# Sums of squares with four columns of ones, and residual products with both halves of the activations in 512 columns

## Chip, core and metric

The kernel runs on one NeuronCore of a Trainium2 chip, as one launch. The metric is the device time of a run in microseconds. In the profile PE is the matrix engine, PEld its loads of the stationary operand, DVE, ACT and POOL the vector, scalar and general engines, SP the engine that issues nearly all transfers.

## What is computed

Two transformer blocks over 256 tokens of 1024 features, in fp32. The first has two layers, each with a feed-forward part, an attention (differential in layer 0, forgetting in layer 1) and a second feed-forward part, all of them added to x with gates from a conditioning vector. The second block adds convolution mixers, a cross-attention to 256 memory tokens and a layer of 16384 experts chosen by product keys. What matters here, cut from the reference:

```python
def rms_norm(x, g):
    y = xf * lax.rsqrt(jnp.mean(xf * xf, axis=-1, keepdims=True) + EPS)
...
def swiglu(h, w_in, w_out):
    g, u = jnp.split(h @ w_in, 2, axis=-1)
    return (jax.nn.silu(g) * u) @ w_out
...
        x = x + 0.5 * g1[:, None, :] * swiglu(h, ffn_w_in[layer, 0], ffn_w_out[layer, 0])
        h = modulate(rms_norm(x, norm_g[layer, 1]), sh2, sc2)
...
        x = x + g2[:, None, :] * mix        # mix ends in  o @ w_o
        h = modulate(rms_norm(x, norm_g[layer, 2]), sh3, sc3)
        x = x + 0.5 * g3[:, None, :] * swiglu(h, ffn_w_in[layer, 1], ffn_w_out[layer, 1])
...
    merged = jax.nn.sigmoid(gate_sc) * y_sc + jax.nn.sigmoid(gate_cf) * y_cf
    return jnp.einsum('bsd,de->bse', merged, w_mix_out)
```

So each product with an output weight (w_out, w_o, w_mix_out, w_xo) is added to x, and the mean square of the new x over its 1024 features is needed before the next norm.

## The kernel before

x lies feature-major in xT, eight tiles of 128 features by 256 tokens. Weights come once each, in chunks of [128, 2048] fp32 (1 MB) into `raw`. Each half of a chunk is split into a rounded part `whi` by ACT (L115) and the remainder `wlo` by DVE (L116), four buffers of each. Activations are kept as such pairs too. A product is `mm3` (L146 to 149): whi with the rounded activations, whi with their remainder, wlo with the rounded ones, each a matmul of 256 columns into one PSUM bank, the weights being the stationary operand.

An output tile n of ffn_out takes 22 such triples (one for each tile of the 2816 hidden features); of a_w_o, b_w_o, w_mix_out and w_xo it takes 8. `residual` (L425) then makes one DVE instruction that multiplies the bank by the gate and adds it to xT (L426); `residual2` (L784) adds without a gate. Behind it `Stat.add` (L180) squares the new tile on ACT (sq, L182), and `Norm.add` (L235) makes the next norm's input: hi on ACT (L237), lo on DVE (L238).

`Stat` sums squares over features. Seven of the eight squared tiles are added up by POOL (sqa, six adds, L193). Then PE multiplies that sum, and after it the eighth tile, with ones (L177): the squares are the stationary operand, 128 columns of ones the moving one, and the first matmul takes 256 columns to clear the bank. The result has tokens on the partitions, the same value in all columns; column 0 alone is read (L198). There are nine such Stats: one behind each residual projection and a second one in the last ffn. Three Stats (memory, first x, convolution LayerNorm) have `on_pe` and send all eight tiles to PE. From the sums come rstd on ACT and DVE, a transposition on PE (`along_row`, L215, tile pt) and the scaling of the norm (L264). The first products behind a residual (`Norm.pair`, L246) use the unscaled input, so that they need not wait for rstd.

In differential attention TF is a Toeplitz tile of the relative bias: eight transfers (L588) read shifted windows of `gneg`, and PE flips them in pairs of heads (L610) before the scores. Beside all that DVE and ACT work off modulation products (araw, L358) as background.

The order of instructions on each engine is set by the framework's scheduler, which goes by its own estimate of durations; each engine then takes its row in that order and waits where an operand is late. PSUM banks and tile buffers rotate in pools.

Of the kernel before, what the change touches and what calls it, by code (L numbers as in the profile page):

```python
# [27 lines left out]
NB = 32  # L28
LAM0 = 0.8 - 0.6 * math.exp(-0.3 * 0)

# ---- columns of the packed per-feature vectors: name -> (first column, count)
# [22 lines left out]
def forward(ctx: ExitStack, tc: tile.TileContext, io, out, tap=None):  # L54
# [21 lines left out]
    # ---------------------------------------------------------------- constants  # L76
# [15 lines left out]
    # ---------------------------------------------------------------- weights  # L92
    class Weights:
        """Streams [128, 2048] chunks; each gives two pieces split exactly into hi + lo."""
# [5 lines left out]
        def pieces(self, src, n=2048, whole=(), loads=1):  # L100
            """whole: pieces that stay plain fp32, for PE's own (slower) fp32 product."""
# [43 lines left out]
    def mm3(o, a, b, start, stop):  # L145
        """o += a.T @ b for operands split into (hi, lo)."""  # L146
        pe.matmul(o, a[0], b[0], start=start, stop=False)  # L147
        pe.matmul(o, a[0], b[1], start=False, stop=False)  # L148
        pe.matmul(o, a[1], b[0], start=False, stop=stop)  # L149

    def tok(h, k, a=0, b=T):
        """tokens a .. b of feature tile k."""
        return h[0][:, k, a:b], h[1][:, k, a:b]
# [4 lines left out]
    def split_into(pair_hi, pair_lo, src, func=AF.Copy, **kw):  # L158
        """exact hi + lo of src (an fp32 SBUF tile)."""
# [3 lines left out]
    # ---------------------------------------------------------------- norms  # L163
    class Stat:
        """Sum of squares over the features: tokens on partitions, then 1 / rms again along the row."""

        def __init__(self, on_pe=False):
            self.ps = bank("po", [128, 2, 128])
# [4 lines left out]
        def sum(self, sq, first, last_):  # L173
            # the first product also clears the other half of the bank
            for t in range(2):
                o, b = (self.ps, ones0) if first and t == 0 else (self.ps[:, t, :], ones)
# [3 lines left out]
        def add(self, ap, scale=1.0):  # L180
# [5 lines left out]
            elif self.k == KT:  # L186
                self.sum(self.acc, True, False)
                self.sum(sq, False, True)
# [13 lines left out]
        def rstd_after(self, r1):  # L202
            """1 / rms of the rows that r1 scales."""
# [7 lines left out]
    def along_row(r):  # L211
        """[token, 2] -> the same values along the tokens of every partition."""
# [9 lines left out]
    class Norm:  # L222
        """h = (src * a) * r + b in hi + lo, in place of src * a, which the first products take:
        they need no r, which is multiplied into what they give (two more columns carry b)."""
# [21 lines left out]
        def pair(self, p0, p1, keep=None):  # L246
            """two output tiles [128, T] in SBUF; then h is what it should be."""
# [29 lines left out]
    def fm_pair(p0, p1, h):  # L277
        """two feature-major output tiles [128, T]; k outermost."""
# [31 lines left out]

    def proj_tm(W, src, h, dst, scale=None):
        """token-major projection of one chunk (256 columns): dst [128, 2, 256]."""
# [13 lines left out]
    # ---------------------------------------------------------------- inputs  # L326
# [20 lines left out]
    # ---------------------------------------------------------------- modulation  # L347
# [45 lines left out]
    # ---------------------------------------------------------------- memory keys and values  # L393
# [31 lines left out]
    def residual(n, o, s, st, norm):  # L425
        dve.scalar_tensor_tensor(xT[:, n, :], o, s, xT[:, n, :], op0=ALU.mult, op1=ALU.add)  # L426
# [3 lines left out]
    # ---------------------------------------------------------------- feed-forward  # L430
# [872 lines left out]
```

## Time and profile before

| what | before |
|---|---|
| median of 3 runs (lowest, highest), us | 2296.33 (2295.49, 2296.72) |
| span of the profiled execution, us | 2292.8 |
| PE busy, share of the span | 98% |
| DVE, ACT, POOL busy | 76%, 55%, 3% |
| DMA | 461.26 MB read, 202 GB/s over the span |
| lines 147, 148, 149 (mm3) in the chain that ended last | 22% each |

The span is that of one profiled execution; the time of a run holds a few microseconds around it. A matmul's duration is modelled and overlaps with the next one's, so the distance from start to start counts, not the duration. A timeline row joins neighbours that are alike: it gives the first start, the time from there to the last end, and the count. The bracket at the end of a row is the idle time of the engine ahead of it and what ended it. In the busy-time view PEclk is the granted clock as a share of full speed.

### The profile page before, as it was taken

How to read it: one execution, taken by the hardware profiler on the slowest of the kernel's cores; microseconds unless marked ns; L12 is line 12 of the kernel's file. 1: busy time of each engine (PE TensorE's matmuls, PEld its weight loads, DVE VectorE, ACT ScalarE, POOL GpSimd, SP SyncE). 2: the span in 40 equal slices, each digit the busy share in tenths (PEclk: the TensorE clock that was granted, in tenths of full speed). 3: DMA queues.
4: the chain of work that ended last, by engine and by line, in shares of the span. 5: the costliest groups of instructions: out<-in, count | busy, mean ns of one | idle time of the engine just before them, and what ended most of it. 6: DMA issues, size and time to landing. Idle time of an engine off the chain costs nothing.

```text
span 2292.8 us, 42711 instructions
## 1 busy us (share of the span) xinstructions
PE 2235.5 (98%) x16756; PEld 2133.5 (93%) x16756; DVE 1739.7 (76%) x3503; ACT 1257.1 (55%) x2389; POOL 72.0 (3%) x75
## 2 busy tenths in 40 slices
PE   8999869999999999999999999999999999999998
PEld 8999858999999999999999999999999999888886
DVE  7877727977877777855699886899668998666665
ACT  5544538644564447644533455545567776555554
POOL 0000100100200010100100000000000000000000
PEclk9999979999999999999999999999999999999999
DMA  9777664677667773455444543245543444555554
GB/s 367 297 295 294 208 138 170 234 299 279 230 266 297 293 292 129 169 202 183 167 164 166 184 181 151 95 184 184 184 166 132 145 148 148 184 190 194 185 185 155
DMA packets 66489, 466.15 MB, mean 203 GB/s; under 512 B 7472, under 2 KB 8944, under 8 KB 10480
## 3 DMA queue, kind: packets, MB, share of 16 engines
q1 hardware_dynamic: 66000, 462.90, 55.4%
q8 instruction: 132, 2.16, 0.4%
q14 instruction: 69, 0.57, 0.1%
q10 hardware_dynamic: 288, 0.52, 0.1%
HBM read 461.26 MB, written 1.05 MB: 202 GB/s over the span
## 4 chain that ended last, share of the span: by engine, by line
PE 90%; DVE 3%; ACT 3%; issue 1%; SPq 1%; DMA 1%; POOL 0%; DVEq 0%; ACTq 0%; POOLq 0%
PE mm L149 22%; PE mm L147 22%; PE mm L148 22%; PE mm L1164 8%; PE lg L1164 8%; PE lg L1114 2%; PE mm L289 2%; SPq L588 1%; PE po L177 1%; DVE wlo L116 1%; ACT whi L115 1%; DMA TF<-gneg 1%; DVE lo L275 0%; DVE lo L238 0%; DVE nt L270 0%
## 5 line engine op out<-in xcount | busy, mean ns | idle before, releaser
L116 DVE TENSOR_TENSOR wlo<-raw,whi 128x1024 fp32r<-128x1024 f32 x696 | 850.1, 1226 | 325.2 <-ACT whi L115 323.7
L115 ACT ACTIVATE whi<-raw 128x1024 fp32r<-128x1024 f32 x696 | 734.3, 1059 | 617.9 <-PE mm L148 411.9
L147 PE MATMUL mm<-hi,whi 128*128 128x256 f32 x3144 | 899.3, 287 | 0.9 <-ACT hi L274 0.6
L149 PE MATMUL mm<-hi,wlo 128*128 128x256 f32 x3144 | 891.7, 284 | 1.4 <-DVE wlo L116 1.1
L148 PE MATMUL mm<-lo,whi 128*128 128x256 f32 x3144 | 886.1, 282 | 0.6 <-DVE lo L275 0.5
L149 PEld LDWEIGHTS mm<-hi,wlo 128*128 128x128 f32 x3144 | 595.4, 189 | 3.0 <-DVE wlo L116 2.7
L148 PEld LDWEIGHTS mm<-lo,whi 128*128 128x128 f32 x3144 | 595.6, 189 | 2.6 <-DVE lo L275 1.2
L147 PEld LDWEIGHTS mm<-hi,whi 128*128 128x128 f32 x3144 | 594.4, 189 | 2.6 <-ACT hi L274 0.8
L149 PE MATMUL mm<-ghi,wlo 128*128 128x256 f32 x704 | 197.7, 281 | 0.0
L147 PE MATMUL mm<-ghi,whi 128*128 128x256 f32 x704 | 197.7, 281 | 0.0
L148 PE MATMUL mm<-glo,whi 128*128 128x256 f32 x704 | 197.7, 281 | 0.0
L358 DVE CUSTOM_DVE_ANT_0 araw<-araw,cb 128x1024 f32<-128x1024 f32 x160 | 190.3, 1218 | 1.0 <-ACT cb L407 1.0
L160 ACT ACTIVATE vph<-S 128x128 fp32r<-128x128 f32 x256 | 77.1, 302 | 133.0 <-PE lg L1164 132.9
L148 PEld LDWEIGHTS mm<-glo,whi 128*128 128x128 f32 x704 | 132.8, 189 | 0.0
L147 PEld LDWEIGHTS mm<-ghi,whi 128*128 128x128 f32 x704 | 132.8, 189 | 0.0
L149 PEld LDWEIGHTS mm<-ghi,wlo 128*128 128x128 f32 x704 | 132.8, 189 | 0.0
L161 DVE TENSOR_TENSOR vpl<-S,vph 128x128 fp32r<-128x128 f32 x256 | 73.5, 288 | 44.3 <-PE lg L1164 44.2
L812 DVE SCALAR_TENSOR_TENSOR cfc<-cf,vec,cfc 128x256 f32<-128x256 f32 x240 | 99.1, 472 | 0.0
L1106 DVE TENSOR_SCALAR ohA<-cst,sel 128x128 f32<-128x128 f32 x256 | 82.2, 342 | 21.8 <-PE lg L1114 20.9
L1164 PE MATMUL mm<-whi,vph 128*128 128x512 f32 x256 | 80.3, 395 | 0.2 <-ACT vph L160 0.2
L1164 PE MATMUL lg<-whi,vpl 128*128 128x512 f32 x256 | 80.5, 395 | 0.0
L1164 PE MATMUL mm<-wlo,vph 128*128 128x512 f32 x256 | 80.5, 395 | 0.0
(387 smaller groups left out, 3279.7 us busy)
## 6 DMA issues: line engine op xcount, KB each, us to landing
raw<-ffn_in SPq DMA_DIRECT2D x88, 1024.0 KB, 4.8
araw<-ada SPq DMA_DIRECT2D x72, 1024.0 KB, 6.8
raw<-peer_u SPq DMA_DIRECT2D x64, 1024.0 KB, 4.8
raw<-peer_v SPq DMA_DIRECT2D x64, 1024.0 KB, 4.8
raw<-ffn_out SPq DMA_DIRECT2D x44, 1024.0 KB, 4.8
araw<-kv_ada SPq DMA_DIRECT2D x8, 1024.0 KB, 6.9
raw<-w_cf SPq DMA_DIRECT2D x8, 1024.0 KB, 4.8
raw<-w_scx SPq DMA_DIRECT2D x8, 1024.0 KB, 4.8
```

Source lines behind the costliest of these rows:

```text
L115: act.activation(hi[:, :m], r, AF.Copy)
L116: last_split[0] = dve.tensor_tensor(lo[:, :m], r, hi[:, :m], op=ALU.subtract)
L147: pe.matmul(o, a[0], b[0], start=start, stop=False)
L148: pe.matmul(o, a[0], b[1], start=False, stop=False)
L149: pe.matmul(o, a[1], b[0], start=False, stop=stop)
L160: act.activation(pair_hi, src, func, **kw)
L161: dve.tensor_tensor(pair_lo, src, pair_hi, op=ALU.subtract)
L289: pe.matmul(o, p[0][:, k * 128:(k + 1) * 128], h32[:, k, :], start=(k == 0), stop=(k == KT - 1))
L358: dve.tensor_tensor_reduce(out=raw[:, i, :], in0=raw[:, i, :], in1=cb, scale=1.0, scalar=0.0, op0=ALU.mult, op1=ALU.add, accum_out=acc[:, ...
L812: dve.scalar_tensor_tensor(o, cf[:, i, j:j + T], w, o, op0=ALU.mult, op1=ALU.add)
L1106: dve.tensor_scalar(A, iota, sel3[:, 0, t:t + 1], sel3[:, 2, t:t + 1], op0=ALU.is_equal, op1=ALU.mult)
L1164: pe.matmul(acc[t][d], lh, rh[:, d * 512:(d + 1) * 512], start=s0, stop=s1)
```

## The change

Sums: the moving operand of a sum has NS = 4 columns of ones (8 in the first matmul, four of them zero) where it had 128 (256). In Stats without on_pe POOL adds up only the first five squared tiles (four adds); tiles 5, 6 and 7 go to PE one by one, so there are 8 matmuls to a Stat instead of 4.

Products: where a projection is added to x, rounded part and remainder of an activation tile now lie side by side (tiles g, oh2, mx), and `mm_wide` gives whi a moving operand of 512 columns, rounded part and remainder, into the two halves of a bank; wlo with the rounded part (256 columns) goes into the first half. `residual` and `residual2` add the two halves to xT one after the other: 48 more instructions of L426's kind and 16 more of L784's. w_mix_out's first two tiles are interleaved, as `proj_fm` did with wide=True. Some tiles are packed otherwise and TF is allocated larger to fit oh2's buffer; the rest of the computation stays.

```diff
+NS = 4
+DIRECT = 5
@@ Stat
-            self.ps = bank("po", [128, 2, 128])
+            self.ps = bank("po", [128, 2, NS])
...
-                o, b = (self.ps, ones0) if first and t == 0 else (self.ps[:, t, :], ones)
+                o, b = (self.ps, ones0[:, 128 - NS:128 + NS]) if first and t == 0 else (
+                    self.ps[:, t, :], ones[:, :NS])
...
-            elif self.k == KT:
-                self.sum(self.acc, True, False)
-                self.sum(sq, False, True)
+            elif self.k > DIRECT:
+                if self.k == DIRECT + 1:
+                    self.sum(self.acc, True, False)
+                self.sum(sq, False, self.k == KT)
@@ new
+    def mm_wide(o, a, b, first, last):
+
+        def cross():
+            pe.matmul(o[:, 0, :], a[1], b[:, 0, :], start=False, stop=False, skip_group_check=True)
+
+        if not first:
+            cross()
+        pe.matmul(o, a[0], b, start=first, stop=last, skip_group_check=True)
+        if first:
+            cross()
@@ new
+    def proj_wide(W, name, g, consume, together=False):
+
+        src = io[name]
+        for c in range(src.shape[0]):
+            it = W.pieces(src[c])
+            if together and c == 0:
+                p = [next(it), next(it)]
+                o = [mm_bank([128, 2, T]) for _ in p]
+                for k in range(KT):
+                    for oo, pp in zip(o, p):
+                        mm_wide(oo, blk(pp, k), g[:, k], k == 0, k == KT - 1)
+                for i in range(2):
+                    consume(2 * c + i, o[i])
+            else:
+                for i, p in enumerate(it):
+                    o = mm_bank([128, 2, T])
+                    for k in range(KT):
+                        mm_wide(o, blk(p, k), g[:, k], k == 0, k == KT - 1)
+                    consume(2 * c + i, o)
+            tick()
@@ residual
-        dve.scalar_tensor_tensor(xT[:, n, :], o, s, xT[:, n, :], op0=ALU.mult, op1=ALU.add)
+        for i in range(2):
+            dve.scalar_tensor_tensor(xT[:, n, :], o[:, i, :], s, xT[:, n, :], op0=ALU.mult, op1=ALU.add)
@@ ffn
-            ghi = fp.tile([128, FKT, T], F32R, name="ghi")
-            glo = fp.tile([128, FKT, T], F32R, name="glo")
+            g = fp.tile([128, FKT, 2, T], F32R, name="g")
...
-                split_into(ghi[:, j, :], glo[:, j, :], pr)
+                split_into(g[:, j, 0, :], g[:, j, 1, :], pr)
...
-                    mm3(o, next(wb), (ghi[:, k, :], glo[:, k, :]), k == 0, k == FKT - 1)
+                    mm_wide(o, next(wb), g[:, k], k == 0, k == FKT - 1)
@@ differential attention
-        proj_fm(W, "a_w_o", (ohi, olo), lambda n, o: residual(n, o, s[:, n:n + 1], st, norm))
+        proj_wide(W, "a_w_o", oh2, lambda n, o: residual(n, o, s[:, n:n + 1], st, norm))
@@ forgetting attention
-        proj_fm(W, "b_w_o", (ohi, olo), lambda n, o: residual(n, o, s[:, n:n + 1], st, norm))
+        proj_wide(W, "b_w_o", oh2, lambda n, o: residual(n, o, s[:, n:n + 1], st, norm))
@@ residual2
-        dve.tensor_tensor(xT[:, n, :], o, xT[:, n, :], op=ALU.add)
+        for i in range(2):
+            dve.tensor_tensor(xT[:, n, :], o[:, i, :], xT[:, n, :], op=ALU.add)
@@ convolution mixers, cross-attention
-        proj_fm(W, "w_mix_out", (mhi, mlo), lambda n, o: residual2(n, o, st, norm), wide=True)
+        proj_wide(W, "w_mix_out", mx, lambda n, o: residual2(n, o, st, norm), together=True)
...
-        proj_fm(W, "w_xo", (ohi, olo), lambda n, o: residual2(n, o, st, norm))
+        proj_wide(W, "w_xo", oh2, lambda n, o: residual2(n, o, st, norm))
```

The scheduler's order shifts in places. Line numbers in the rows of the changed kernel are its own: L107 is there what L105 was, L118 what L116, L253 what L238, L394 what L358, L463 what L426, L623 what L588; L156 is the 256-column matmul of mm_wide, L160 the one of 512.

SP's row in differential attention, before and then changed; TF are the transfers of the relative bias, raw the weight chunks.

```order
L105 DMA raw<-a_q 128x2048
L355 DMA araw<-ada 128x2048
L105 DMA raw<-a_k 128x2048
L588 DMA TF<-gneg 128x1x256 x8
L105 DMA raw<-a_v 128x2048
```

```order
L107 DMA raw<-a_q 128x2048
L391 DMA araw<-ada 128x2048
L623 DMA TF<-gneg 128x1x256 x8
L107 DMA raw<-a_k 128x2048
L107 DMA raw<-a_v 128x2048
```

The eight TF transfers have moved ahead of the a_k chunk, which now stands between them and a_v.

DVE's row in a_w_o up to the weight split for output tile 6, the last row of each; ahead of the first piece stand two L426 rows and one split of this projection, ahead of the second five L463 rows, one split and two of L253.

```order
L238 SCALAR_TENSOR_TENSOR lo<-xT,mod_sc_4213,hi 128x256 x2
L426 SCALAR_TENSOR_TENSOR xT<-mm,mod_gt_2625,xT 128x256
L116 TENSOR_TENSOR wlo<-raw,whi 128x1024
L426 SCALAR_TENSOR_TENSOR xT<-mm,mod_gt_2625,xT 128x256
L358 ISA araw,acc_gt_4556<-araw,cb 128x1024
L358 ISA acc_gt_4556 128x1
L238 SCALAR_TENSOR_TENSOR lo<-xT,mod_sc_4213,hi 128x256
L358 ISA araw,acc_gt_4556<-araw,cb 128x1024
L358 ISA acc_gt_4556 128x1
L238 SCALAR_TENSOR_TENSOR lo<-xT,mod_sc_4213,hi 128x256
L426 SCALAR_TENSOR_TENSOR xT<-mm,mod_gt_2625,xT 128x256
L116 TENSOR_TENSOR wlo<-raw,whi 128x1024
```

```order
L463 SCALAR_TENSOR_TENSOR xT<-mm,mod_gt_2547,xT 128x256 x2
L118 TENSOR_TENSOR wlo<-raw,whi 128x1024
L253 SCALAR_TENSOR_TENSOR lo<-xT,mod_sc_4043,hi 128x256
L463 SCALAR_TENSOR_TENSOR xT<-mm,mod_gt_2547,xT 128x256
L394 ISA araw,acc_gt_4346<-araw,cb 128x1024
L394 ISA acc_gt_4346 128x1
L463 SCALAR_TENSOR_TENSOR xT<-mm,mod_gt_2547,xT 128x256
L394 ISA araw,acc_gt_4346<-araw,cb 128x1024
L394 ISA acc_gt_4346 128x1
L253 SCALAR_TENSOR_TENSOR lo<-xT,mod_sc_4043,hi 128x256
L463 SCALAR_TENSOR_TENSOR xT<-mm,mod_gt_2547,xT 128x256 x2
L118 TENSOR_TENSOR wlo<-raw,whi 128x1024
```

Behind the same splits, eleven L463 instructions in all now precede the last row, where five of L426 did.

PE's row at the end of b_w_o, before and then changed; sqa is the sum of squares that POOL made, boh (bohi, bolo) the attention's output.

```order
L149 MATMUL mm<-bohi,wlo 128x256
L147 MATMUL mm<-bohi,whi 128x256
L148 MATMUL mm<-bolo,whi 128x256
L149 MATMUL mm<-bohi,wlo 128x256
L177 MATMUL po<-ones_70,sqa 128x256
L177 MATMUL po<-ones_70,sqa 128x128
L147 MATMUL mm<-hi,whi 128x258
L148 MATMUL mm<-lo,whi 128x258
L149 MATMUL mm<-hi,wlo 128x258
L147 MATMUL lg<-hi,whi 128x258
```

```order
L160 MATMUL mm<-boh,whi 128x512
L156 MATMUL mm<-boh,wlo 128x256
L160 MATMUL mm<-boh,whi 128x512
L156 MATMUL mm<-boh,wlo 128x256
L160 MATMUL mm<-boh,whi 128x512
L156 MATMUL mm<-boh,wlo 128x256
L191 MATMUL po<-ones_70,sqa 128x8
L191 MATMUL po<-ones_70,sqa 128x4
L160 MATMUL mm<-boh,whi 128x512
L156 MATMUL mm<-boh,wlo 128x256
L160 MATMUL mm<-boh,whi 128x512
L156 MATMUL mm<-boh,wlo 128x256
```

Before, the sum of POOL's squares stands behind the last product of the projection; now it stands inside the product of an earlier tile (tile 6), two 4-column matmuls with 512-column ones before and after it.

## Rows read from the trace of the kernel before

**Rows 1.** The page, parts 1 and 4: busy us (share) xinstructions; share of the chain.

```profile
PE 2235.5 (98%) x16756; PEld 2133.5 (93%) x16756; DVE 1739.7 (76%) x3503; ACT 1257.1 (55%) x2389; POOL 72.0 (3%) x75
...
PE 90%; DVE 3%; ACT 3%; issue 1%; SPq 1%; DMA 1%; POOL 0%; DVEq 0%; ACTq 0%; POOLq 0%
```

**Rows 2.** Busy time by stretch, the second ffn_out: columns in the first row.

```profile
core 0: us, PE busy (x) PEld busy (x) DVE busy (x) ACT busy (x) POOL busy (x), PEclk, DMA share, GB/s
...
549.00:611.66 62.66, 62.66 (x530) 62.66 (x529) 47.67 (x61) 30.29 (x39) 7.31 (x6) 1.00 0.71 269
```

**Rows 3.** Timeline of PE in the peer value stage: start, us, engine, line, instructions.

```profile
2199.83 0.62 PE L1164 MATMUL lg<-wlo,vph 128*128 128x512 f32 x2
...
2202.62 0.62 PE L1164 MATMUL lg<-wlo,vph 128*128 128x512 f32 x2
```

**Rows 4.** Timeline of PE at the end of the first ffn.

```profile
259.01 0.82 PE L177 MATMUL po<-ones,sqa 128*128 128x256 f32 x4
259.59 0.37 PE L147 MATMUL mm<-hi,whi 128*128 128x258 f32 x1
...
260.57 0.71 PE L177 MATMUL po<-ones,sq 128*128 128x128 f32 x4
261.04 0.37 PE L147 MATMUL mm<-hi,whi 128*128 128x258 f32 x1
```

**Rows 5.** Timeline of PE at the sums of squares of the convolution LayerNorm.

```profile
1308.80 4.05 PE L177 MATMUL po<-ones,sq 128*128 128x256 f32 x32
1312.60 0.36 PE L149 MATMUL mm<-yhi,wlo 128*128 128x256 f32 x1
```

**Rows 6.** Timeline of PE at L677, a first look and a longer one.

```profile
645.21 0.23 PE L677 MATMUL lg<-cst,zb 16*128 16x16 f32 x1 [1.26 <-DVE zb L673]
...
645.21 0.29 PE L677 MATMUL lg<-cst,zb 16*128 16x16 f32 x2 [1.26 <-DVE zb L673]
```

**Rows 7.** Lines L426 and L238 on DVE: count, ns minimum/median/maximum, first and last start.

```profile
L426 DVE SCALAR_TENSOR_TENSOR xT<-mm,mod_gt,xT x48: 469/479/487, 204.4 to 1130.7; 128x256 f32<-128x256 f32 x48
...
L238 DVE SCALAR_TENSOR_TENSOR lo<-xT,mod_sc,hi x32: 472/953/1803, 205.8 to 939.8; 128x256 fp32r<-128x256 f32 x32
```

**Rows 8.** Timeline of DVE in a_w_o.

```profile
411.05 0.47 DVE L426 SCALAR_TENSOR_TENSOR xT<-mm,mod_gt,xT 128x256 f32<-128x256 f32 x1
411.44 1.21 DVE L116 TENSOR_TENSOR wlo<-raw,whi 128x1024 fp32r<-128x1024 f32 x1
```

**Rows 9.** Timeline of PE in a_w_o and at b_w_o's end, [idle before <-releaser].

```profile
412.71 0.38 PE L149 MATMUL mm<-ohi,wlo 128*128 128x256 f32 x1 [0.98 <-DVE wlo L116]
...
938.15 1.31 PE L177 MATMUL po<-ones,sqa 128*128 128x256 f32 x4 [1.84 <-POOL sqa L193]
```

**Rows 10.** Busy time by stretch (columns as in rows 2): TF, projections, mixers.

```profile
283.00:317.50 34.50, 10.65 (x22) 5.51 (x23) 1.61 (x4) 2.39 (x4) 0.00 (x0) 0.51 0.81 84
401.00:424.00 23.00, 20.96 (x170) 20.25 (x170) 22.14 (x33) 14.72 (x26) 5.94 (x6) 1.00 0.47 181
918.00:943.00 25.00, 23.16 (x181) 22.84 (x181) 21.40 (x30) 15.64 (x26) 6.04 (x6) 0.93 0.42 151
938.50:942.00 3.50, 3.50 (x17) 3.41 (x16) 1.86 (x4) 1.08 (x3) 0.00 (x0) 0.51 0.41 126
1351.00:1382.00 31.00, 30.96 (x260) 30.70 (x260) 25.82 (x37) 19.55 (x31) 6.82 (x6) 1.00 0.56 202
```

**Rows 11.** Timeline of PE at the flips of TF.

```profile
286.59 2.05 PE L610 MATMUL lg<-TF,cst 128*128 128x512 f32 x2 [6.27 <-DMA TF<-gneg]
...
305.78 2.05 PE L610 MATMUL lg<-TF,cst 128*128 128x512 f32 x2 [7.56 <-DMA TF<-gneg]
...
313.85 2.04 PE L610 MATMUL lg<-TF,cst 128*128 128x512 f32 x2 [5.81 <-DMA TF<-gneg]
```

**Rows 12.** Timeline of SP: start, us in the queue's issue, transfer.

```profile
273.41 0.33 SPq L105 DMA_DIRECT2D raw<-a_k  x1
274.09 27.80 SPq L588 DMA_DIRECT2D TF<-gneg  x8
```

More of the change, by code (lines that the diff above doesn't have):

```diff
@@ L467, in ffn @@
             for n in range(KT):
-                o = mm_bank([128, T])
+                o = mm_bank([128, 2, T])
                 for k in range(FKT):
-                    mm3(o, next(wb), (ghi[:, k, :], glo[:, k, :]), k == 0, k == FKT - 1)
+                    mm_wide(o, next(wb), g[:, k], k == 0, k == FKT - 1)
                 residual(n, o, s[:, n:n + 1], st, nxt)
@@ L490, in forward @@
         TB = ap_.tile([128, 8, 256], F32, name="TB")
-        olo = ap_.tile([128, 8, 256], F32R, name="olo")
         qk = {}
@@ L561, in a_out @@
                 pe.transpose(pt[:, t * 128:(t + 1) * 128], o[:, t, :], ident)
-            act.activation(ohi[:, hd, :], pt, AF.Copy, scale=g08)
-            dve.scalar_tensor_tensor(olo[:, hd, :], pt, g08, ohi[:, hd, :], op0=ALU.mult, op1=ALU.subtract)
+            act.activation(oh2[:, hd, 0, :], pt, AF.Copy, scale=g08)
+            dve.scalar_tensor_tensor(oh2[:, hd, 1, :], pt, g08, oh2[:, hd, 0, :], op0=ALU.mult, op1=ALU.subtract)
         def a_v(c):
@@ L584, in forward @@
                 dve.scalar_tensor_tensor(gneg, pf, -1.0, mrow, op0=ALU.mult, op1=ALU.add)
-                TF = ap_.tile([128, 8, 256], F32, tag="ohi", name="TF")
+                TF = ap_.tile([128, 16, 256], F32, tag="ohi", name="TF")
                 for hd in range(8):
@@ L611, in forward @@
                     act.activation(TB[:, 2 * q:2 * q + 2, :], pb, AF.Copy)
-                ohi = ap_.tile([128, 8, 256], F32R, tag="ohi", name="ohi")
+                oh2 = ap_.tile([128, 8, 2, 256], F32R, tag="ohi", name="oh2")
             if g < 3:
@@ L702, in forward @@
         h = norm.scaled_by(st).h
-        ohi = ap_.tile([128, KT, 256], F32R, name="bohi")
-        olo = ap_.tile([128, KT, 256], F32R, name="bolo")
+        oh2 = ap_.tile([128, KT, 2, 256], F32R, name="boh")
         mask = ap_.tile([128, 256], F32, name="mask")
@@ L750, in b_pair @@
                 pe.transpose(pt[:, t * 128:(t + 1) * 128], o[:, t, :], ident)
-            act.activation(ohi[:, n, :], pt, AF.Copy)
-            dve.tensor_tensor(olo[:, n, :], pt, ohi[:, n, :], op=ALU.subtract)
+            act.activation(oh2[:, n, 0, :], pt, AF.Copy)
+            dve.tensor_tensor(oh2[:, n, 1, :], pt, oh2[:, n, 0, :], op=ALU.subtract)
         for g in range(4):
@@ L837, in scx_evac @@
             step(6)
-        yhi = cp.tile([128, KT, T], F32R, tag="phi", name="yhi", bufs=2)
-        ylo = cp.tile([128, KT, T], F32R, tag="plo", name="ylo", bufs=2)
+        y2 = cp.tile([128, 2, KT, T], F32R, tag="py", name="y2")
+        yhi, ylo = y2[:, 0], y2[:, 1]
         def scb_evac(i, o):
@@ L881, in forward @@
         r = along_row(st.rstd())
-        chi = cp.tile([128, KT, T], F32R, tag="phi", name="chi", bufs=2)
-        clo = cp.tile([128, KT, T], F32R, tag="plo", name="clo", bufs=2)
+        chi = cp.tile([128, KT, T], F32R, name="chi")
+        clo = cp.tile([128, KT, T], F32R, name="clo")
         for i in range(KT):
@@ L889, in forward @@
         proj_fm(W, "sc_w_out", (yhi, ylo), sc_out)
-        mhi = cp.tile([128, KT, T], F32R, tag="phi", name="mhi", bufs=2)
-        mlo = cp.tile([128, KT, T], F32R, tag="plo", name="mlo", bufs=2)
+        mx = cp.tile([128, KT, 2, T], F32R, tag="py", name="mx")
         row = along_row(r1)
@@ L901, in pw2 @@
             dve.tensor_tensor(gcf[:, n, :], gcf[:, n, :], gsc[:, n, :], op=ALU.add)
-            split_into(mhi[:, n, :], mlo[:, n, :], gcf[:, n, :])
+            split_into(mx[:, n, 0, :], mx[:, n, 1, :], gcf[:, n, :])
         proj_fm(W, "cf_w_pw2", (chi, clo), pw2, wide=True)
@@ L915, in forward @@
         pw = ctx.enter_context(tc.tile_pool(name="pw", bufs=1, side="right"))
-        ohi = ap_.tile([128, KT, 256], F32R, name="xohi")
-        olo = ap_.tile([128, KT, 256], F32R, name="xolo")
+        oh2 = ap_.tile([128, KT, 2, 256], F32R, name="xoh")
         qs = {}
@@ L950, in x_head @@
                     pe.matmul(po[:, d, :], xa_v[:, m, c:c + 128], wT[:, m, :], start=(m == 0), stop=(m == 1))
-            act.activation(ohi[:, 2 * hd:2 * hd + 2, :], po, AF.Copy)
-            dve.tensor_tensor(olo[:, 2 * hd:2 * hd + 2, :], po, ohi[:, 2 * hd:2 * hd + 2, :], op=ALU.subtract)
+            o_ = oh2[:, 2 * hd:2 * hd + 2]
+            act.activation(o_[:, :, 0, :], po, AF.Copy)
+            dve.tensor_tensor(o_[:, :, 1, :], po, o_[:, :, 0, :], op=ALU.subtract)
         for g in range(4):
```

## Prediction

> **What bounds the kernel now.** I read the page first. PE is busy in 98% of the span, and the chain that ended last runs through PE for 90% of it [rows 1]; so the kernel is bound by the number and length of matmuls, and by the few places where PE stands. Next come the stretches in which the product of the changed projections runs. The second ffn_out is 528 matmuls of 256 columns in 62.66 us, with PE and its weight loads busy throughout [rows 2]: 118.7 ns from one to the next. No wait is hidden there, so what a matmul gets cheaper goes straight off the time. DVE is busy 47.7 of those 62.66 us, ACT 30.3, POOL 7.3 [rows 2]. The two attention projections look different: around a_w_o DVE is busy 22.14 of 23.00 us, around b_w_o 21.40 of 25.00, around w_mix_out 25.82 of 31.00 [rows 10]. Here extra DVE work has little or no room. Last I looked at the longest standstill of PE: four waits for TF, 5.81 to 7.56 us each, the first flip at 286.59 and the last at 313.85 [rows 11], with the clock at 0.51 for that whole stretch [rows 10].
>
> **Wide products.** A triple was three 256-column matmuls, 3 x 118.7 = 356.1 ns. It becomes one of 256 and one of 512. The peer value stage already runs 512-column matmuls of the same type: 12 of them from 2199.83 to 2202.62, 232.5 ns each [rows 3]. Two of 256 take 237.4, so a triple saves 4.9 ns, the price of one start; the columns streamed are the same. There are 4 x 176 triples in ffn_out: 704 x 4.9 = **-3.4 us**. The 128 triples of w_mix_out and w_xo give **-0.6**. The 128 of the attention projections (-0.3 each) are counted with those stages.
>
> **Sums of squares.** Each fp32 matmul of a sum stands as two records (16 of them give x32 in the trace). At the end of an ffn a Stat took 259.01 to 259.59 and 260.57 to 261.04, 1.05 us for 8 records [rows 4]. Now three tiles go to PE directly: 16 records of 4 (one pair of 8) columns. No row shows 4 columns. The nearest is a 16-column fp32 matmul with a 128-column load: two records, the first lasting 0.23 us and both together 0.29 [rows 6], so ends 60 ns apart; if the columns cost nothing more, 58 is my value. Bounds: 0.05, and upward 119 ns, the mean of the 128-column records (32 in the 3.80 us from 1308.80 to 1312.60 [rows 5]), since fewer columns should not cost more. At 58 a Stat takes 16 x 58 = 0.93 us: -0.12 each. Four ffn Stats and the second Stat of the last ffn: **-0.6**; w_mix_out and w_xo: **-0.2**. The convolution LayerNorm sums every tile on PE: 32 x (119 - 58) = **-1.9**. Its squares come from ACT about every 0.4 us and the new order puts two or three products between them, so I see no new wait. The two opening Stats lie in a stretch that the weight transfers pace; **+0.3** (0 to +1.5) for a clock that may rise later.
>
> By the Trainium skill (TensorE: Matmul & The Clock Gate, section LDWEIGHTS (loading the stationary operand)) a load costs its columns divided by 1.2, which for 128 is an estimate of 107 ns whatever the rows; the sums would then cost about what they cost at 128 columns, and twice the number would be a loss. By [rows 6] the trace speaks against it. I weigh it as the second rival, below, priced from [rows 5].
>
> **TF.** The first fence of the orders shows the eight TF transfers ahead of a 1 MB a_k chunk in SP's queue. Before, a_k was issued at 273.41 and TF from 274.09, taking the queue for 27.80 us [rows 12]. Pairs of TF set the flips: (313.85 - 286.59) / 3 = 9.1 us a pair [rows 11]. The first flip came 12.5 us after the first issue, 3.4 more than a pair. That excess and the 0.7 us of earlier issue are the most that can be won, -4. Against it: 7 more a_v products stand behind the last flip (44 instead of 37), 0.8 us at full clock and 1.6 at half; that is work moved, not added, and matters only by the clock, 0.8. The a_k chunk now waits for the queue as a_v did, and a_v stands behind it. In PE's order the a_k products come after 44 a_v products, the first scores and 48 a_q products, about 11 us behind the last flip, so I give a late chunk +0.8 at most. I take **-1.5**.
>
> **a_w_o.** DVE adds two halves, each 395 ns before the next instruction (411.05 to 411.44 [rows 8]; the 48 of before last 469 to 487 ns each, beside POOL or not [rows 7]): 8 more, +3.2 us on an engine that is idle for 0.9 of 23 us [rows 10]. Two POOL adds fewer relieve the lo splits, which last 472 alone and 953 beside POOL [rows 7]: 2 x 0.48 = -0.9. DVE's row grows by 2.2 us. The second fence shows where it hits: 11 halves (five tiles and one) instead of 5 residuals stand ahead of the wlo split for tile 6, for which PE waited 0.98 us already [rows 9]: 6 x 0.395 = 2.4 later, so PE should wait some 3 us there. The tail to the rstd shifts by as much, and the triples return 0.3. **+2.0**; 0 if the products that wait for no r cover it, +4 if the clock halves again after the wait, as after the 1.84 us wait at b_w_o (3.5 us at 0.51 [rows 10], so 1.75 lost).
>
> **b_w_o.** PE waited 1.84 us for POOL's last add [rows 9] and then ran 3.5 us at half clock [rows 10]: 3.6 us in all. The third fence puts that sum inside tile 6 of the product and leaves the last tiles to direct sums, so this wait goes. Next late is DVE, +2.2 as above; the splits stand early in its row here. -3.6 + 2.2 - 0.3 would be -1.7; since a sum in mid-stage must still wait for POOL, **-1.0** (-3.6 to +1.0).
>
> **w_mix_out, w_xo.** 8 more adds in each, priced as above at 3.2 us; around w_mix_out DVE is idle for 5.2 us [rows 10], and I count w_xo alike. The sum over tiles 0 to 4 now stands at about the end of tile 5 and needs DVE, ACT and POOL in a row first: **+1.0** (0 to +2).
>
> In the ffn_out stages the 32 extra adds fall into 15 us of idle DVE [rows 2], and the sums stand behind later products, so they cost nothing; without that cover they would cost 0.4 each. The 18 fewer POOL adds gain nothing where DVE isn't late.
>
> **Sum.** -3.4 - 0.6 - 0.6 - 0.2 - 1.9 + 0.3 - 1.5 + 2.0 - 1.0 + 1.0 = -5.9 us. The profiled execution has a span of 2292.8 [rows 1] and some 3.5 us outside it, which the change leaves alone; against the median of 2296.33 this gives **2290.4**, -0.26%.
>
> **Rivals.**
> First, a larger gain: TF gives the whole -4, b_w_o -3.0, and a_w_o and the mixers nothing: -5.9 - 2.5 - 2.0 - 2.0 - 1.0 = -13.4, **2282.9**. For it: PE's waits there are real; against it: DVE is full at a_w_o. 0.14.
> Second, the weight load paces the 4-column sums. At 112 to 119 ns a record, 7 Stats cost 16 x 0.112 - 1.05 = +0.74 instead of -0.12, +6.0, and the LayerNorm loses its -1.9 but 0.2: +7.7, **2298.1**. The Trainium skill's rule above is this one. It decides from 66 ns a record, where the 16 records cost more than the 8. The two records of [rows 6] start 83 or less and end 60 apart: 0.12.
> Third, slower: DVE becomes the bound of all four projections. A tile takes PE 8 x 351 = 2.8 us; DVE needs a 1.21 us split [rows 8], a lo of 0.47 to 0.95 [rows 7], two halves of 0.4 and at the attention projections now and then a modulation product (L358): it decides where that exceeds 2.8. a_w_o is there; at the mixers the three come to 2.5 to 2.9. If all four pay 3.2 without relief, and two half clocks of 1.75 follow, that is 16.3, on the -7.9 of the terms outside these stages: +8.4, **2304.7**. 0.08.
> Fourth, it doesn't do what it says: a 512-column matmul that reads two interleaved halves streams no quicker than two of 256. Then -4.0 goes: **2294.4**. The 512-column matmuls of [rows 3] read one plain stretch, and that is all that speaks for it. 0.06.
>
> **How the numbers follow.** The forecast keeps 0.60, and its own range is 2286.5 to 2293.5 by the bounds of a_w_o, TF and the sums. A measurement of this kernel can tell about 0.2% (4.6 us), so faster means below 2291.7 and slower above 2300.9. Faster: five sixths of the forecast and the first rival, 0.52 + 0.14 = 0.66; same: the rest of the forecast and the second and fourth, 0.26; slower: the third, 0.08. From 2284 to 2297.5 leaves out the third rival, half of the first and most of the second's upper side, about 2 in 10.
>
> **What would show it.** Wide products: ffn_out stages 0.85 us shorter each, L160 records 232 ns apart. Sums: records of 4 columns about 58 ns apart, the LayerNorm's part 1.9 us shorter. TF: the last flip 1.5 to 3 us earlier against the end of the ffn before it. a_w_o: a PE wait for wlo near tile 6 of 2.5 to 3.2 us, DVE without a gap. b_w_o: no wait of 1.8 us on POOL and no half clock behind. The forecast is wrong if the 4-column records stand 80 ns or more apart, if a_w_o costs over 4 us, or if the a_k chunk behind TF stops PE.

## The result

The changed kernel takes 2322.19 us (2319.72 to 2323.70), beside 2296.07 us for the kernel before: a ratio of 1.0114, 95% interval 1.0102 to 1.0127. I had forecast 2290.4 and at most 2297.5. It is 26 us slower.

The profiled execution has a span of 2317.9 us, 25 more than before. These rows are from the page of the changed kernel (parts 1 and 4, as [rows 1]):

```profile
PE 2249.4 (97%) x15868; PEld 2100.3 (91%) x15868; DVE 1760.1 (76%) x3567; ACT 1257.8 (54%) x2389; POOL 61.4 (3%) x57
...
PE 90%; DVE 4%; ACT 2%; SPq 1%; DMA 1%; issue 1%; POOL 0%; POOLq 0%; DVEq 0%; ACTq 0%
```

And these from the waits of its PE: line, what it waited for, us in total, times, the longest.

```profile
PE po L191 <- POOL sqa L208: 5.9, 4, 2.0
PE mm L151 <- DVE wlo L118: 5.5, 8, 1.2
PE mm L149 <- ACT hi L289: 4.1, 3, 2.4
PE mm L160 <- DVE xT L463: 1.8, 2, 1.3
```

There are 888 matmul records fewer, and PE is busy 14 us longer; so more than half of the 25 us is no wait of this list but matmuls that have become dearer (a lower clock and waits too short for the list count as busy here). The wide products are not the ones. This timeline of PE is from the start of the second ffn_out:

```profile
561.41 0.39 PE L160 MATMUL mm<-g,whi 128*128 128x512 f32 x1
561.64 0.39 PE L156 MATMUL mm<-g,wlo 128*128 128x256 f32 x2
561.88 0.39 PE L160 MATMUL mm<-g,whi 128*128 128x512 f32 x1
562.11 0.28 PE L156 MATMUL mm<-g,wlo 128*128 128x256 f32 x1
```

From L160 to the L156 behind it are 230 ns and back again 118: 348 ns a triple, where I had 351.2 and the three matmuls of before took 356.1. Further on in the same product sums stand between the triples:

```profile
610.97 0.39 PE L160 MATMUL mm<-g,whi 128*128 128x512 f32 x1
611.21 0.50 PE L191 MATMUL po<-ones,sq 128*128 128x4 f32 x4
611.57 0.37 PE L156 MATMUL mm<-g,wlo 128*128 128x256 f32 x1
611.77 0.40 PE L160 MATMUL mm<-g,whi 128*128 128x512 f32 x1
```

The four records of 4 columns take 0.36 us (the first start is 25 ns ahead of the second, the other three steps are 112 ns), and the product behind them takes 0.20 where it takes 0.118 elsewhere. Nothing waits in these rows. At other groups the sums start some 0.17 us late as well, and their four records take 0.47:

```profile
259.21 0.28 PE L156 MATMUL mm<-g,wlo 128*128 128x256 f32 x1
259.50 0.61 PE L191 MATMUL po<-ones,sq 128*128 128x4 f32 x4
259.97 0.48 PE L160 MATMUL mm<-g,whi 128*128 128x512 f32 x1
260.29 0.28 PE L156 MATMUL mm<-g,wlo 128*128 128x256 f32 x1
```

From 259.21 to 260.29 PE spends 1.08 us on two matmuls of a triple, which cost 0.35 alone, and one group of sums: 0.73 for 4 records, where the group at 611.21 costs 0.45. What differs is the square. These are ACT's rows for the two groups:

```profile
259.05 0.40 ACT L196 ACTIVATE sq<-xT 128x256 f32<-128x256 f32 x1
...
610.50 0.42 ACT L196 ACTIVATE sq<-xT 128x256 f32<-128x256 f32 x1
```

The first square ended 0.05 us ahead of its group's first record, the second 0.29. So PE waited for ACT at the first, too shortly for a bracket. All groups behind projections at full clock in this trace are of these two kinds, but for four that wait for POOL: 15 start 0.05 us behind the end of their square, 0.05 to 0.17 late, and take 0.47 us; 14 find it ready, lose at most 0.01 ahead and take 0.36. Behind the group both lose 0.08 to 0.09.

Where the 25 us arise is read from PE's timelines, by the first matmul of each stage: how much longer a part takes than before (an ffn_out ends here with the transposition of rstd). The other columns are profiled executions of experiments told below (wide products alone, three tiles direct alone, 4 columns alone), all against the kernel before. The execution profiled of the wide products alone is the fastest of its ten, 2.3 us under their median, so that column is as much too low.

| part, us more than before | change | wide alone | direct alone | 4 columns alone |
|---|---|---|---|---|
| opening, up to the first ffn_out | +5.0 | -0.1 | -0.1 | +2.7 |
| four ffn_out with the sums and rstd behind | +4.0 | -5.4 | +10.5 | +2.2 |
| a_w_o to the next ffn_out | +7.2 | +4.6 | -0.2 | +0.2 |
| b_w_o to the next ffn_out | +3.9 | -0.9 | +0.2 | +0.1 |
| convolution mixers up to w_mix_out | +0.9 | -0.2 | +0.2 | +1.0 |
| w_mix_out, w_xo and what follows to the end | +5.7 | +2.1 | +5.3 | +1.6 |
| rest (attention with TF, between the stages) | -1.4 | +0.7 | +1.7 | +0.6 |
| sum | +25.2 | +0.8 | +17.6 | +8.4 |

At b_w_o no part alone makes the loss; it comes from their meeting, as told below.

### The profile page after: what moved, and what is told of

Same layout as the page of the kernel before. It is cut to its first block, busy times and chain, and to the rows that moved or that the text cites. A ratio compares the mean times of both kernels' runs of the same rounds, so it can differ in the third digit from the quotient of the medians.

```text
span 2317.9 us, 40895 instructions
## 1 busy us (share of the span) xinstructions
PE 2249.4 (97%) x15868; PEld 2100.3 (91%) x15868; DVE 1760.1 (76%) x3567; ACT 1257.8 (54%) x2389; POOL 61.4 (3%) x57
## 4 chain that ended last, share of the span: by engine, by line
PE 90%; DVE 4%; ACT 2%; SPq 1%; DMA 1%; issue 1%; POOL 0%; POOLq 0%; DVEq 0%; ACTq 0%
PE mm L151 17%; PE mm L149 17%; PE mm L150 17%; PE mm L160 8%; PE mm L1198 8%; PE lg L1198 8%; PE mm L156 4%; PE lg L1148 2%; PE mm L304 2%; PE po L191 1%; DVE wlo L118 1%; SPq L623 1%; DMA TF<-gneg 1%; DVE nt L285 1%; ACT whi L117 1%
## 5 line engine op out<-in xcount | busy, mean ns | idle before, releaser
L118 DVE TENSOR_TENSOR wlo<-raw,whi 128x1024 fp32r<-128x1024 f32 x696 | 850.9, 1226 | 329.8 <-ACT whi L117 327.2
L160 PE MATMUL mm<-g,whi 128*128 128x512 f32 x704 | 244.9, 394 | 0.0
L156 PE MATMUL mm<-g,wlo 128*128 128x256 f32 x704 | 192.1, 280 | 0.0
L394 DVE CUSTOM_DVE_ANT_0 araw<-araw,cb 128x1024 f32<-128x1024 f32 x160 | 190.6, 1221 | 1.0 <-ACT cb L443 1.0
L160 PEld LDWEIGHTS mm<-g,whi 128*128 128x128 f32 x704 | 130.5, 188 | 26.3
L156 PEld LDWEIGHTS mm<-g,wlo 128*128 128x128 f32 x704 | 132.6, 188 | 2.5
L1198 PE MATMUL lg<-whi,vph 128*128 128x512 f32 x256 | 80.4, 395 | 0.0
L1198 PE MATMUL lg<-wlo,vph 128*128 128x512 f32 x256 | 80.3, 395 | 0.0
```

The source lines that it names most:

```text
L118: last_split[0] = dve.tensor_tensor(lo[:, :m], r, hi[:, :m], op=ALU.subtract)
L156: pe.matmul(o[:, 0, :], a[1], b[:, 0, :], start=False, stop=False, skip_group_check=True)
L160: pe.matmul(o, a[0], b, start=first, stop=last, skip_group_check=True)
L394: dve.tensor_tensor_reduce(out=raw[:, i, :], in0=raw[:, i, :], in1=cb, scale=1.0, scalar=0.0, op0=ALU.mult, op1=ALU.add, accum_out=acc[:, ...
L1198: pe.matmul(acc[t][d], lh, rh[:, d * 512:(d + 1) * 512], start=s0, stop=s1)
```

## Experiments

Theory S: the sums cost the time, by the weight load, by their number and place, and by the clock. Theory H: the second half on DVE costs it, at the projections behind attention and mixers.

**The parts alone.** First the wide products without the new sums, an edit of the change:

```diff
-NS = 4
-DIRECT = 5
+NS = 128
+DIRECT = 7
```

> The products in 512 columns as in the change, the sums of squares as before (128 columns of ones, POOL adds seven tiles). Theory S (the sums cost the time: records paced by the weight load, twice as many, placed inside the products, and a lower clock behind them): the triples save about 8 ns each in the four ffn_out stages, about -1.4 us a stage, the attention projections give some of it back; -6 to +3 us in all, 2290 to 2299. Theory H (the second half on DVE costs the time in the projections behind attention and mixers): +10 to +16 us, 2306 to 2312, with PE waiting in a_w_o and b_w_o for xT or wlo.

Measured: 2297.97 us beside 2294.93, ratio 1.0014 (1.0004 to 1.0023), 3.0 us slower: the upper end of what S said, and not the 10 to 16 of H. Each ffn_out is 1.50 us shorter (61.3 us where [rows 2] has 62.66), and the table shows what takes it back: a_w_o, w_mix_out and w_xo.

The next three are edits of the kernel before, with the change's `Stat` and the constants shown.

```diff
+NS = 4
+DIRECT = 5
```

> The sums of squares as in the change (4 columns, three tiles direct), the products as before. Theory S: most of the +26 us, +15 to +26, with 112 ns between 4-column records and the opening 5 us longer at half clock. Theory H: +8 to +12, which is the opening and 0.5 us for each Stat.

Measured: 2320.50 us, ratio 1.0107 (1.0090 to 1.0124), 25.6 us: the sums alone lose as much as the whole change. The places are not all the same: in this trace the LayerNorm's stage ran 6.8 us at half clock (1331.0 to 1337.8), in the changed kernel's it did not.

```diff
+NS = 4
+DIRECT = 7
```

> Only the number of columns changes to 4; POOL still adds seven tiles, so a Stat keeps 4 matmuls and its place. Theory S in the form that the weight load alone sets the pace: 128 and 4 columns cost the same 112 ns, so 0 to -1 us outside the opening. If the narrow matmuls also pull the clock down in the opening, +3 to +6 us there; if the opening is late for another reason (the order), 0.

Measured: 2304.74 us, ratio 1.0049 (1.0032 to 1.0066): 9.8 us for nothing but fewer columns. That is more than any of my three cases, the largest being 3 to 6 us in the opening.

```diff
+NS = 128
+DIRECT = 5
```

> Only the number of tiles that go to PE directly changes (three), with 128 columns of ones. Theory S: 8 more records of 112 ns in each of nine Stats, +0.9 us each or +8 us, plus waits for POOL or ACT inside the products, +8 to +14; the opening unchanged. Theory H: below +8, since sums inside a stage would be hidden by waits that are there anyway.

Measured: 2312.51 us, ratio 1.0076 (1.0059 to 1.0093), 17.6 us, where S said 8 to 14. The two parts nearly add up (9.8 + 17.6 = 27.4, together 25.6). S holds against H, with both parts dearer than it said. In ffn_out a group with 128 columns reads like one with 4 (its line is L180):

```profile
244.91 0.28 PE L151 MATMUL mm<-ghi,wlo 128*128 128x256 f32 x1
245.29 0.71 PE L180 MATMUL po<-ones,sq 128*128 128x128 f32 x4
245.76 0.36 PE L149 MATMUL mm<-ghi,whi 128*128 128x256 f32 x1
245.96 0.28 PE L150 MATMUL mm<-glo,whi 128*128 128x256 f32 x1
```

0.47 us for the four records, 0.26 more than usual ahead of them, 0.08 behind. Here too the 0.26 is the square:

```profile
244.82 0.42 ACT L185 ACTIVATE sq<-xT 128x256 f32<-128x256 f32 x1 [1.75 <-DVE xT L430]
```

It ended at 245.24, 0.05 us ahead of the group.

**The price of a record.** A probe behind the last product of the kernel before, with constants only:

```diff
+            pb = bank("po", [128, 128])
+            for k_, m_, n_ in ((128, 128, 128), (128, 128, 4), (128, 128, 128), (128, 32, 4), (128, 128, 128),
+                               (16, 128, 4)):
+                for _ in range(48):
+                    with tc.issue_after(last_mm.ins):
+                        last_mm = pe.matmul(pb[:m_, :n_], ident[:k_, :m_], ones[:k_, :n_], start=True, stop=True)
```

Of each triple the first number is the rows, the second the stationary columns, the third the moving ones.

> Behind the last product six runs of 48 fp32 matmuls on constants: stationary 128x128 with 128 moving columns, with 4, with 128, stationary 128x32 with 4, 128x128 with 128, stationary of 16 rows by 128 columns with 4. Theory S (the load of 128 stationary columns sets the pace): 112 ns a record in all but the 32-column one, which goes at about 28 to 40; the 16-row one at 112 too. My prediction's estimate: 58 ns for the 4-column ones. Does the clock fall within the runs of 4 columns and not within those of 128? Theory S with the clock says yes.

Measured, in timelines of about 1 us from the first, second, second again, fourth, sixth and sixth run. The row's time runs to the end of its last record, and the 32 columns stand in `128*32`:

```profile
2289.81 1.39 PE L1171 MATMUL po<-ones,cst 128*128 128x128 f32 x11
2295.76 1.48 PE L1171 MATMUL po<-ones,cst 128*128 128x4 f32 x12
2304.82 1.42 PE L1171 MATMUL po<-ones,cst 128*128 128x4 f32 x6
2323.83 1.31 PE L1171 MATMUL po<-ones,cst 128*32 128x4 f32 x37
2337.84 1.36 PE L1171 MATMUL po<-ones,cst 16*128 16x4 f32 x11
2344.71 1.63 PE L1171 MATMUL po<-ones,cst 16*128 16x4 f32 x7
```

And the busy time of PE in the same stretches (PEclk is the first number behind the bracket):

```profile
2290.00:2291.00 1.00, 1.00 (x11) 1.00 1.11 387
2296.00:2297.00 1.00, 1.00 (x12) 1.00 0.00 0
2305.00:2306.00 1.00, 1.00 (x6) 0.50 0.00 0
2324.00:2325.00 1.00, 1.00 (x37) 1.00 0.06 16
2338.00:2339.00 1.00, 1.00 (x11) 1.00 0.00 0
2345.00:2346.00 1.00, 1.00 (x7) 0.50 0.00 0
```

At full clock a record comes every 112 ns with 128 moving columns and every 112 ns with 4; from 16 rows also every 112; with 32 stationary columns every 32. So with 4 moving columns the stationary ones set the pace, and rows don't count; 128 moving columns cost no more. The Trainium skill (TensorE: Matmul & The Clock Gate, section LDWEIGHTS (loading the stationary operand)) puts the load of the stationary operand at its columns divided by 1.2, whatever its rows: by estimate 107 ns for 128 columns and 27 for 32. The trace agrees within some 5 ns, with 112 and 32. The second and the sixth run fall to a clock of 0.50, 1.2 of 2.4 GHz, while PE is busy without a gap, and a record then takes 213 ns; the first and the fifth run, of 128 columns, stay at 1.00, and the third, of 128 columns, comes back to it. Four moving columns cost no less than 128 here, and in both runs of them the clock fell.

**Which narrow sums cost it.** In the kernel before, 4 columns only where a Stat sums every tile on PE:

```diff
-            self.ps = bank("po", [128, 2, 128])
+            self.n = NS if on_pe else 128
+            self.ps = bank("po", [128, 2, self.n])
...
```

> 4 columns only in the three Stats that sum every tile on PE (memory, first x, convolution LayerNorm); the nine others with 128 columns and two sums. If the loss with 4 columns alone (+8 to +10) comes from these (the clock rises later behind the memory sums, falls behind those of x, and the LayerNorm's rstd is later): +6 to +9. If it comes from the nine others and the shifted order: 0 to +2.

Measured: 2303.54 us beside 2295.65, ratio 1.0032 (1.0020 to 1.0044), 7.9 us beside the 9.8 of 4 columns everywhere. The places differ, though: here 4.3 us arise up to the first ffn_out and 5.4 from the last ffn_out to w_mix_out, there 2.7 and 2.2; so this run alone doesn't show how much of the 9.8 these three Stats make. Its stretch at the convolution LayerNorm (columns as in [rows 2]):

```profile
1312.00:1316.50 4.50, 4.42 (x38) 4.19 (x36) 2.77 (x8) 2.73 (x7) 0.00 (x0) 1.00 0.67 233
1316.50:1327.00 10.50, 10.50 (x51) 10.50 (x52) 2.14 (x4) 4.21 (x6) 0.00 (x0) 0.51 0.00 1
```

Here PE ran 10.5 us at half clock behind the interleaved sums, though it never stood. In the changed kernel the LayerNorm's sums don't do this. The opening is alike wherever these Stats have 4 columns (five traces, the changed kernel's among them): PE's records come at the pace of full clock from 15.7 to 19.0 us on, and at 42.9 to 44.2 the clock falls to 0.50 for 3.4 or 6.8 us. With 128 columns (nine traces) full clock comes at 8.7 to 11.8, and there is no such fall there.

**Price against place.** In the kernel before, three tiles direct with 128 columns, but all sums behind the product:

```diff
+            self.direct = 5
+            self.late = []
...
-            elif self.k == KT:
-                self.sum(self.acc, True, False)
-                self.sum(sq, False, True)
+            elif self.k > self.direct:
+                self.late.append(sq)
+                if self.k == KT:
+                    self.sum(self.acc, True, False)
+                    for q in self.late:
+                        self.sum(q, False, q is sq)
...
```

> Three tiles go to PE directly, with 128 columns, but their matmuls stand together behind the last product of the projection (in 7 of the 9 Stats; the two of the last ffn stay as before). If the price of the extra records alone made the loss: 8 records of 112 ns in 7 Stats, +6 us, 2300 to 2303. If the place inside the products made it (waits for ACT and POOL, a bubble before and after every group): near 0 to +3. If the last sum now stands ahead of the next products and waits for its square: +9 to +13.

Measured: 2300.22 us, ratio 1.0019 (1.0010 to 1.0028), 4.6 us. 56 records of 112 ns cost 6.3 in these 7 Stats; in this trace PE's waits for POOL's sum are gone, 2.7 us before, and waits of 1.0 us for squares have come. Inside the products the same sums cost 17.6 us in 9 Stats, and their 72 records are 8.1 of it, so more than half is not the records. What it is can be counted in part, from PE's timeline with three direct tiles alone, in the Stats behind projections and against the kernel before: +8.7 us for the records and the 0.08 behind each group, +1.8 for squares that come late, +0.5 for POOL, 11 in all. The other 6.7 stand outside the sums. Of these 1.25 is a wait for wlo at 1479.4 and 1.7 the half clock from 1480.4 to 1483.8; how they hang on the sums is not shown, and the rest is open.

**From the change's side.** The on_pe Stats back at 128 columns:

```diff
-            self.ps = bank("po", [128, 2, NS])
+            self.n = 128 if on_pe else NS
+            self.ps = bank("po", [128, 2, self.n])
...
```

> The whole change, but the three Stats that sum every tile on PE keep 128 columns. Theory S with the clock: the opening and the convolution LayerNorm get back what they lost, -7 to -11 against the change, 2311 to 2316. Without an effect of the narrow columns on the clock: -2 to 0, 2320 to 2323.

Measured: 2316.34 us, ratio 1.0095 (1.0079 to 1.0110): 5.9 us less than the change, or 4.8 by what each is above the kernel before beside it; short of the 7 to 11 expected. The products of the memory values start as early as in the kernel before again (40.9 us, in the change 46.1).

```diff
-DIRECT = 5
+DIRECT = 7
```

> The whole change, but POOL adds seven tiles again, so a Stat has its two sums behind the products. Theory S: three direct tiles alone cost +17 us, so -14 to -18 against the change, 2304 to 2309. If the waits they bring are hidden by the wide products' own: -5 to -8, 2314 to 2317.

Measured: 2305.44 us, ratio 1.0050 (1.0035 to 1.0066): 16.8 us less than the change, or 15.7 by what each is above the kernel before beside it, as S said.

**What takes back the wide products' gain.** An edit of the run with the wide products alone: DVE adds only the first half (in `residual` and `residual2`):

```diff
-        for i in range(2):
+        for i in range(1):
```

> The wide products everywhere with the sums of before, but DVE adds only the first half of each bank; the second half (rounded weights with the remainder of the activations) is left out of x. The run with both adds is +3 us against the kernel before, though the four ffn_out give -6. If the second add on DVE is what takes that back around a_w_o and at the mixers: -6 to -8, 2287 to 2290, and PE's waits for xT and wlo in a_w_o gone. If it is the wide matmuls or the order: +1 to +4 still.

Measured: 2292.52 us beside 2294.98, ratio 0.9988 (0.9979 to 0.9997), 2.5 us faster than before, where both adds are 3.0 slower. That lies between the two cases expected. So the second add is worth 5.5 of the 9 us by which the wide products miss the gain of the ffn_out. PE's waits for DVE's xT and wlo in a_w_o with both adds, then with one:

```profile
PE mm L160 <- DVE xT L463: 1.8, 2, 1.3
PE mm L151 <- DVE wlo L118: 1.2, 1, 1.2
...
PE mm L156 <- DVE wlo L118: 0.7, 1, 0.7
```

```profile
PE mm L156 <- DVE wlo L118: 1.8, 1, 1.8
PE mm L151 <- DVE wlo L118: 1.1, 1, 1.1
```

The waits for a bank (xT) go, those for wlo grow from 1.9 to 2.9 us, in another order of DVE's row. With one add a_w_o is still 3.4 us slower than before in its profile, 1.7 of it by a half clock from 432.8 to 436.2; what else keeps it slow is open.

**A faster kernel.** Wide products where they stand in a dense stage, sums as before. In ffn_out alone:

```diff
-                o = mm_bank([128, T])
+                o = mm_bank([128, 2, T])
                 for k in range(FKT):
-                    mm3(o, next(wb), (ghi[:, k, :], glo[:, k, :]), k == 0, k == FKT - 1)
-                residual(n, o, s[:, n:n + 1], st, nxt)
+                    mm_wide(o, next(wb), g[:, k], k == 0, k == FKT - 1)
+                residual(n, [o[:, 0], o[:, 1]], s[:, n:n + 1], st, nxt)
...
```

> The products in 512 columns in the four ffn_out stages only; the four other projections and all sums as before. Theory S, refined by the run with the wide products alone (-1.50 us in each ffn_out, +4.6 around a_w_o, +2 at the mixers and w_xo): -6 us, 2288 to 2291. Theory H in its wider form (extra DVE adds cost wherever they are): 2293 to 2297, no gain.

Measured: 2289.88 us beside 2295.65, ratio 0.9971 (0.9960 to 0.9983), 5.8 us faster. And in ffn_out and b_w_o, the further edit:

```diff
-        proj_fm(W, "b_w_o", (ohi, olo), lambda n, o: residual(n, [o], s[:, n:n + 1], st, norm))
+        proj_wide(W, "b_w_o", oh2, lambda n, o: residual(n, [o[:, 0], o[:, 1]], s[:, n:n + 1], st, norm))
...
```

> Wide products in the four ffn_out and in b_w_o, sums as before. In the run with wide products everywhere b_w_o's stage gained about 0.9 us: -6 to -7.5 in all, 2288 to 2290, hardly to be told from wide products in ffn_out alone (-5.8). If b_w_o pays for the second add as a_w_o does: -1 to -4.

Measured: 2289.50 us beside 2294.98, ratio 0.9975 (0.9966 to 0.9985), 5.5 us faster, a little short of the 6 to 7.5 expected. Both beat the kernel before by some 5.6 us, and can't be told from each other.

## Why the prediction was wrong

The step that failed is the price of a 4-column record. I took 58 ns from the ends of two records at L677 [rows 6], the only narrow matmuls of the trace. The probe shows 112, in its sixth run also with the 16 rows and 128 stationary columns of that pair. A pair can't show a pace: its ends are modelled, and in the changed kernel the first step of a group at full clock is 25 to 30 ns where the square was ready and some 130 behind a wait; 112 is the step from the second record on. On that pair I set aside the rule of the Trainium skill (TensorE: Matmul & The Clock Gate, section LDWEIGHTS (loading the stationary operand)), which goes by the columns. The second rival, at 0.12, was the right one in kind, but its time, 2298.1, is still 24 us short. Two things were missing from it, which I had put at nothing or nearly so.

- **Place.** I costed a sum by its records alone and held that in ffn_out it lies behind products and costs nothing more. Nothing covers it there: its records lengthen the product, each group loses 0.08 us behind it, and a group whose square is only just ready 0.1 to 0.4 more. Three tiles direct cost 17.6 us in place and 4.6 at the end of the product (in 9 and in 7 Stats); of the 17.6, 11 are found at the sums themselves.
- **Clock.** I had seen that a clock may rise later in the opening, at +0.3 (0 to +1.5). The opening lost 5.0. The rows show it, changed kernel then before, at nearly one time: 0.41 us for a 256-column record is half clock, 0.28 full.

```profile
13.90 0.41 PE L151 MATMUL mm<-mhi,wlo 128*128 128x256 f32 x1
```

```profile
13.89 0.28 PE L148 MATMUL mm<-mlo,whi 128*128 128x256 f32 x1
```

During and behind the sums of x it falls again (busy time in the changed kernel, PEclk 0.80 and 0.86; the last row is the kernel before, at 1.00):

```profile
37.00:47.00 10.00, 9.28 (x68) 8.93 (x66) 3.93 (x10) 5.89 (x11) 0.00 (x0) 0.80 0.94 384
47.00:57.00 10.00, 9.79 (x71) 9.73 (x72) 9.55 (x14) 4.48 (x6) 0.00 (x0) 0.86 0.53 203
...
37.00:47.00 10.00, 9.06 (x73) 8.62 (x72) 6.50 (x10) 5.66 (x9) 0.00 (x0) 1.00 0.78 310
```

The other steps:

- **Wide products, right in kind, small in size.** -3.4 us for ffn_out; alone they gave -1.50 in each, -6.0, since a triple saves 8.5 ns where I had 4.9. The fourth rival falls.
- **Sums at the ffn, -0.6.** They cost: with the products' -5.4 taken off, the ffn_out row of the table leaves +9.4.
- **LayerNorm, -1.9.** The mixers up to w_mix_out took 0.9 us more; at 112 ns a record there was nothing to gain: the 119 of [rows 5] holds the start of its long group, and the steps within it are 112 as well.
- **TF, -1.5.** Right where I looked, and no use. The lag against before shrinks from 5.6 us at the end of the first ffn to 3.8 behind the last flip, and is 5.2 at a_w_o's start. It is given back in the products behind the flips. The a_k chunk behind TF stopped nothing: PE has no wait for it.
- **a_w_o, +2.0 (0 to +4).** +7.2, of which the wide products alone make 4.6. The wait is not the one I named. PE didn't wait for wlo of tile 6 but, twice, for a bank whose halves DVE had not yet added, then for POOL's sum, now inside the product:

```profile
418.93 0.47 PE L160 MATMUL mm<-oh,whi 128*128 128x512 f32 x1 [1.32 <-DVE xT L463]
...
420.94 0.61 PE L191 MATMUL po<-ones,sqa 128*128 128x8 f32 x4 [1.31 <-POOL sqa L208]
```

  I had counted the second add as DVE time but forgotten that a bank is free only behind it. The clock fell twice there (0.57 in 421.5 to 425.5 and in 438.5 to 442.5), which I had as one end of the range. The direct sums make little of this: with POOL's seven tiles back the stretch costs 6.4 us, and the clock falls twice there too (0.50 from 418.4 to 421.8 and from 435.5 to 438.9).
- **b_w_o, -1.0.** +3.9. With wide products alone it is -0.9, which meets the forecast by luck: PE still waits 1.5 us for POOL, and most of the gain is a clock that did not fall in that execution. With the new sums the wait for POOL [rows 9] didn't go but moved inside the product, and the half clock with it (0.52 from 947.5 to 951.0):

```profile
946.14 0.61 PE L191 MATMUL po<-ones,sqa 128*128 128x8 f32 x4 [1.97 <-POOL sqa L208]
```

  Both cost about what they cost before (1.84 us [rows 9] and 3.5 us at 0.51 [rows 10]), so the +3.9 is elsewhere. PE waits behind b_w_o for the scaled input of the next ffn, ahead of which DVE's row now has a weight split (PE's row, then two of DVE's):

```profile
962.31 0.39 PE L149 MATMUL mm<-hi,whi 128*128 128x256 f32 x1 [2.41 <-ACT hi L289]
...
960.10 1.22 DVE L118 TENSOR_TENSOR wlo<-raw,whi 128x1024 fp32r<-128x1024 f32 x1 [1.92 <-ACT whi L117]
961.24 0.86 DVE L285 SCALAR_TENSOR_TENSOR nt<-xT,mod_sc,pt 128x256 f32<-128x256 f32 x2
```

  That wait, 2.41 us, stands neither in the trace of the wide products alone nor in that of three direct tiles alone; it comes with both together, in an order of DVE's row that the kernel before doesn't have.

- **w_mix_out and w_xo, +1.0.** +5.7 to the end; +5.3 with three tiles direct alone and +2.1 with the wide products alone, so more from the sums than from DVE's adds. Of the 5.3, 1.25 and 1.7 are the wait for wlo and the half clock named above, which stand behind the last sum.
- **The third rival** (DVE as the bound of all four projections) had the right sign, at 2304.7, by the wrong engine: DVE's second add costs 5.5 us, and the sums 25.6.

## What to carry to other kernels

Count a small matmul by its stationary operand before its moving one: with 128 stationary columns, 4 moving columns cost here what 128 cost, so more such instructions are more time. A sum that leaves another engine's queue must still find a place on PE, and inside a dense product it costs more than its own length. Where a group starts late without a bracket, look at when its operand was ready: a short wait hides in the modelled durations. Widen moving operands where a stage is dense and the engine that empties the bank has time; it was worth 0.25 to 0.3% here.

## What the runs showed of the hardware

- A record of an fp32 matmul takes 112 ns at full clock with 128 stationary columns, for 128 or 4 moving columns and (at 4) for 128 or 16 rows, and 32 ns with 32 stationary columns and 4 moving ones.
- In the probe the granted clock fell from 1.00 to 0.50 in both runs of 96 records with 4 moving and 128 stationary columns, without a gap on PE, and a record took 213 ns; in two runs with 128 moving columns and the same pace it stayed at 1.00, and in a third it came back to it.
- Behind a group of fp32 sums the next fp32r product takes 0.08 to 0.09 us longer. Ahead of a group PE loses at most 0.01 us where the square is ready; a group whose square ended 0.05 us earlier starts 0.05 to 0.17 us late in the changed kernel, and its four records take 0.47 instead of 0.36.
- A 512-column and a 256-column matmul in turn come at 230 and 118 ns.
